# Grouped mixture of experts on one core: the branch to further passes moved behind the last scatter, weight splits ordered ahead of the last copies on ScalarE too, and three of four embedding quarters kept in routing

## The chip, the cores and the metric

The kernel runs on one core of one Trainium2 chip. Its time is the device time of one execution in microseconds (us), and less is better. Before the change it takes 1997.78 us, the median of 3 runs (1997.4 to 1998.72).

The engines are TensorE (PE, with PEld for its weight loads), VectorE (DVE), ScalarE (ACT), GpSimd (POOL) and SyncE (SP, which issues the DMA loads). A "q" behind an engine's name in a profile (PEldq, SPq) means its sequencer: branches, register loads, semaphores and DMA issues, which are not counted as busy.

## What is computed

A float32 network over S = 256 tokens of width D = 1024. A first block of two layers is followed by a second block of four. The change touches only the feed-forward half of the first block's two layers:

```python
for i in range(2):
    mix = ...                       # S5 and pooling in layer 0, attention in layer 1
    x = layer_norm(ALPHA * x + mix, ...)
    ple = (p[i] @ ple_w_proj[i]) * sigmoid(x @ ple_w_gate[i])     # the "embedding"
    ffn = grouped_moe(x, router_w, router_bias, w1[i], w3[i], w2[i])
    x = layer_norm(ALPHA * x + ffn + ple, ...)
```

`grouped_moe` scores 16 experts for each token, chooses a group of four, and in it the two best experts, and adds their `(silu(x w1) * (x w3)) w2`, weighted by the scores. w1 and w3 are 1024 x 512 and w2 is 512 x 1024 for each expert, so a layer reads 96 MB of expert weights.

## The kernel before, in words

**Routing.** `moe` first calls `route` (the scores) and `choose` (L1276), which finds the chosen experts (`Mb`, L1314), counts by five small matmuls (L1318 to L1322) how many tokens each expert has so far, and makes from that each token's `slot` in its expert (L1336, L1337) and its `gates` (L1339 to L1342). An expert takes CAP = 64 tokens in one pass. `choose` also works out the number of passes that the fullest expert needs (`cn`, `npass`, `ni`, L1324 to L1334). `values_load` (L1545) puts `ni` into a register of every engine (one TENSOR_LOAD on each), and `further_passes` (L1596) holds an `If` on it (L1600): a COMPARE_BRANCH on each engine, behind which the loops of the second and later passes stand. With these inputs no further pass is needed, so every engine jumps over them. All this lies ahead of the first expert.

**Embedding.** While routing goes on, PE computes a quarter of the columns of `x @ ple_w_gate` in four pieces of 4 matmuls (`embed`, L1513; one piece is 8 records of the profile), two of them ahead of `choose` and two behind. The tanh and the products behind it are `th` (L1518) on ACT and `pp` (L1521, L1523) on DVE. In this text a piece of 4 is called an embedding quarter.

**Experts.** The 16 experts go in four batches of four. `onehot` (L1349) makes from `slot` the matrix `oh` that selects a batch's tokens; `gather` multiplies it with the tokens (L1363, 16 pairs of records) and copies the result (`xl`, L1365). For each expert `expert_in` does the w1 and w3 products (L1394; its result `h` is copied by ACT, L1397), `expert_act` transposes, takes the silu and the gate (L1405 to L1411). For each pair of experts `pair_out` does the w2 products (L1431) into two halves, copies each half as a high part on ACT (`y`, L1437) and a low part on DVE (L1438), and `scatter` (L1445) adds it to the accumulators `acc` by matmuls. The accumulators are zeroed ahead of the branch by four matmuls (L1543).

**Layer norm.** Behind the last scatter `layer_norm` takes the statistics of `acc` on DVE (L783 to L789, which end in `dg` and `h`); `transpose_part` transposes by PE (L1099), with the bias as a matmul of its own (`bz`, L1092) and matmuls on a tile of ones (L1090) ahead.

**Weights.** Loads of one MB (L109) go into a ring of 16 slots. Three slots are other tiles lent out once: `gb`, `y` and `h`. The next stage's weights are loaded and split ahead of the last scatter by `run_ahead` (L97): each MB is cut in two pieces, and of each piece ACT writes the high part (L122) and DVE the low part (L123). These are 6 splits in layer 0 and 4 in layer 1.

**Order.** A scheduler sets the order of each engine's instructions from priorities; `issue_after(m)` keeps an instruction behind `m`. `run_ahead` returns its last split, `s.split_last`, which is the DVE's, and `pair_out` keeps its last copies behind it: that holds DVE's two `y` copies back, while ACT's two go first. On SP, 14 weight loads are issued ahead of the branch from a list (`s.feed`), the loads into `y`, `gb` and `h` behind it.

Of the kernel before, what the change touches and what calls it, by code (L numbers as in the profile page):

```python
# [8 lines left out]
F32 = mybir.dt.float32  # L9
# [21 lines left out]
class Net:  # L31
    def __init__(s, ctx, tc, ins):
        s.ctx, s.tc, s.nc, s.ins = ctx, tc, tc.nc, ins
        s.right = ctx.enter_context(ExitStack())
        s.slots = [c.enter_context(tc.tile_pool(name="slots" + n, bufs=1, side="right")) for c, n in ((ctx, "a"), (s.right, "b"))]
        s.zpool = None

        s.ahead = deque()

        s.feed = deque()  # L40
# [71 lines left out]
    def split(s, v, to=None):  # L112
# [5 lines left out]
        for i0 in range(0, a, m):  # L118
# [3 lines left out]
            nc.scalar.activation(h, v[:, i0:i0 + n], AF.Copy)  # L122
            s.split_last = nc.vector.tensor_tensor(l, v[:, i0:i0 + n], h.bitcast(F32), op=OP.subtract).ins  # L123
# [1152 lines left out]
    def choose(s, sc, pool, token_rest):  # L1276
# [46 lines left out]
        cn = T([128, 2], "cn")  # L1323
        nc.vector.tensor_reduce(cn[:, 0:1], pr[:, 32:48], axis=AX.X, op=OP.max)  # L1324
        ts(cn[:, 1:2], cn[:, 0:1], 1.0 / CAP, (CAP - 1) / CAP, op0=OP.mult, op1=OP.add)

        npass = T([128, 4], "npass")
        for k in range(3):
            ts(npass[:, k:k + 1], cn[:, 0:1], float(CAP * (k + 1)), None, op0=OP.is_gt)
        tt(npass[:, 0:1], npass[:, 0:1], npass[:, 1:2], op=OP.add)  # L1330
        ts(npass[:, 0:1], npass[:, 0:1], 1.0, None, op0=OP.add)
        tt(npass[:, 0:1], npass[:, 0:1], npass[:, 2:3], op=OP.add)
        ni = T([128, 1], "ni", I32)
        nc.vector.tensor_copy(ni, npass[:, 0:1])  # L1334
# [7 lines left out]
        tt(gates, gates, red[:, :, 0:1].to_broadcast([128, 2, 16]), op=OP.mult)  # L1342
        token_rest(1)
        return gates, slot, ni
# [69 lines left out]
    def pair_out(s, w2, a, wk, last=None, n=2, ahead=None):  # L1414
# [20 lines left out]
        with s.tc.issue_after(ahead()) if ahead else ExitStack():  # L1435
# [51 lines left out]
    def moe(s, i, x, ahead):  # L1487
# [4 lines left out]
        part = lambda w, n, q: w[q * n * 128:(q + 1) * n * 128].rearrange("(a p) n -> p a n", p=128)  # L1492
        both = lambda a, b, n: (lambda q: [s.feed.popleft() if s.feed else s.load(part(w, n, q)) for w in (a, b)])
        with ExitStack() as stack:
# [51 lines left out]
            next(em)  # L1546
            s.further_passes(reg, slot, gates, acc, (w1, w3, w2), pool, wk)
            s.ring["w"].extendleft([gate, lambda: s.hp.tile([128, 2048], F32, name="h"), lambda: pool.tile([128, 2048], F32, name="gb"),
                                    lambda: wk.tile([128, 2048], F32, name="y", bufs=1)])
            nxt = batch(0, oh)  # L1550
            for _ in em:
                pass
            done, acts, y = [], [], None
            for e in range(NE):
# [3 lines left out]
                h = s.expert_in(both(w1[e], w3[e], 4), xg[:, :, q], wk)  # L1558
                if q == 0:
# [24 lines left out]
                if e == 12:  # L1584
                    lnr = s.norm_rows(lnz, pool, False)
# [5 lines left out]
            s.scatter(acc, y, done.pop(0), False, True)  # L1591
            x = s.layer_norm(acc, lnr, True, s.cols["mix_norm"] if i else None)
# [3 lines left out]
    def further_passes(s, reg, slot, gates, acc, w, pool, wk):  # L1596
# [3 lines left out]
        with s.tc.If(reg > 1):  # L1600
            left = wk.tile([128, 2, 16], F32, name="left", bufs=1)
            nc.vector.tensor_copy(left, slot)
            with s.tc.For_i(1, reg):
                nc.vector.tensor_scalar(left, left, float(CAP), None, op0=OP.subtract)
                with s.tc.For_i(0, NE, 2) as e:
                    sl = wk.tile([128, 2, 2, 2], F32, name="sl")
                    nc.vector.tensor_copy(sl[:, 0], left[:, :, bass.ds(e, 2)])
                    nc.vector.tensor_copy(sl[:, 1], gates[:, :, bass.ds(e, 2)])
                    oh = s.onehot(sl[:, 0], s.hp.tile([128, 2048], F32, name="h")[:, :4 * CAP].bitcast(F32R), 2)
                    xg, rest = s.gather(oh, lambda: pool.tile([128, 2048], F32, name="gb")[:, :4 * CAP].rearrange("p (t c) -> p t c", t=2), sl[:, 1], wk)  # L1610
                    oT, gr = rest()

                    def pair(a, b, n):

                        def get(q):
                            m = pool.tile([128, 2048], F32, name="gb").rearrange("p (z a n) -> z p a n", z=2, a=n)
# [370 lines left out]
```

## Time and profile before

| | us |
|---|---|
| median of 3 runs | 1997.78 |
| the profiled execution | 1997.02 |
| its span on the core | 1995.3 |
| TensorE busy in the span | 1943.9 (97%) |
| VectorE busy | 1045.9 (52%) |
| ScalarE busy | 794.0 (40%) |
| GpSimd busy | 90.1 (5%) |

The span is what the trace covers, from the first to the last instruction; the profiled execution's own time is 1.72 us longer, and it lies 0.76 us below the median. The mean granted TensorE clock was 0.99 of full speed. A group of the trace gives its start, its duration, the engine, the line, the operation and tiles, and in square brackets how long the engine stood idle before it and what ended that. Matmuls in float32 are recorded as two records each.

### The profile page before, as it was taken

To read this page: it belongs to the slowest core of one execution; us is meant where nothing else is said; L and a number is where in the kernel's file an instruction comes from. 1 tells how busy PE (TensorE), PEld (TensorE's weight loads), DVE (VectorE), ACT (ScalarE), POOL (GpSimd) and SP (SyncE) were. 2 spreads that over 40 slices of the span, in tenths; PEclk is the share of its full clock that TensorE was granted. 3 is DMA by queue.
4 is the path that set the end of the run, shared out by engine and by line. 5 is a ranking of instruction groups with operands and counts; after the bars stand their busy time and mean duration, and the time that the engine had idled before them with its cause. 6 is when DMAs were issued, how large, how long until landed. Compare 5 with 4: busy or idle time off the path is not lost.

```text
span 1995.3 us, 29243 instructions
## 1 busy us (share of the span) xinstructions
PE 1943.9 (97%) x12088; PEld 1508.1 (76%) x12088; DVE 1045.9 (52%) x1707; ACT 794.0 (40%) x1194; POOL 90.1 (5%) x109
## 2 busy tenths in 40 slices
PE   8999999989999999899999999999999999999999
PEld 6664444378754543499999998999878999999998
DVE  8951111065441111486655698555686555757554
ACT  4321111144321111355444597444655444535442
POOL 5300000000000000000000000000140000000000
PEclk9999999989999999999999999999999999999999
DMA  8559999843679999484655545554453555555540
GB/s 250 186 217 389 390 389 396 307 161 101 207 274 393 389 393 393 141 291 139 222 188 190 174 161 178 190 190 125 151 169 127 190 188 180 180 171 190 184 133 22
DMA packets 271598, 444.34 MB, mean 223 GB/s; under 512 B 14354, under 2 KB 165185, under 8 KB 271457
## 3 DMA queue, kind: packets, MB, share of 16 engines
q1 hardware_dynamic: 270192, 442.30, 63.7%
q8 instruction: 98, 1.61, 0.3%
q14 instruction: 44, 0.35, 0.1%
q10 hardware_dynamic: 1264, 0.09, 0.0%
HBM read 441.30 MB, written 1.05 MB: 222 GB/s over the span
## 4 chain that ended last, share of the span: by engine, by line
PE 64%; DVE 3%; ACT 2%; POOL 1%; issue 1%; DMA 0%; POOLq 0%; ACTq 0%; DVEq 0%; SPq 0%
PE mm L177 11%; PE mm L175 11%; PE mm L176 11%; PE mm L1394 6%; PE acc L175 5%; PE acc L176 5%; PE acc L177 5%; PE mm L1431 3%; PE mm L1513 1%; DVE z L123 1%; PE acc L1445 1%; PE mm L1363 1%; POOL hrs L536 1%; DVE e L417 1%; PE mm L240 0%
## 5 line engine op out<-in xcount | busy, mean ns | idle before, releaser
L123 DVE TENSOR_TENSOR z<-w,z 128x1024 fp32r<-128x1024 f32 (+1 forms) x382 | 453.0, 1204 | 277.7 <-ACT z L122 277.5
L175 PE MATMUL mm<-xh,z 128*128 128x256 f32 x1920 | 540.4, 282 | 0.0
L177 PE MATMUL mm<-xh,z 128*128 128x256 f32 x1920 | 539.0, 281 | 0.4 <-DVE z L123 0.4
L176 PE MATMUL mm<-xl,z 128*128 128x256 f32 x1920 | 538.7, 281 | 0.2
L122 ACT ACTIVATE z<-w 128x1024 fp32r<-128x1024 f32 (+1 forms) x382 | 389.3, 1045 | 288.4 <-PE mm L177 141.3
L175 PEld LDWEIGHTS mm<-xh,z 128*128 128x128 f32 x1920 | 362.1, 189 | 3.4 <-ACT z L122 1.1
L176 PEld LDWEIGHTS mm<-xl,z 128*128 128x128 f32 x1920 | 361.4, 188 | 3.7 <-DVE xl L1121 1.6
L177 PEld LDWEIGHTS mm<-xh,z 128*128 128x128 f32 x1920 | 362.1, 189 | 2.5 <-DVE z L123 2.5
L1394 PE MATMUL mm<-w,xl 128*64 128x512 f32 x1008 | 237.4, 596 | 0.0
L175 PE MATMUL acc<-z,yh 128*128 128x512 f32 x488 | 195.1, 400 | 0.5 <-ACT yh L216 0.5
L176 PE MATMUL acc<-z,yh 128*128 128x512 f32 x488 | 193.7, 397 | 0.0
L177 PE MATMUL acc<-z,yl 128*128 128x512 f32 x488 | 193.0, 397 | 0.0
L1394 PEld LDWEIGHTS mm<-w,xl 128*64 128x64 f32 x1008 | 72.3, 137 | 136.2 <-issue 131.7
L1431 PE MATMUL mm<-w,ea 128*64 128x512 f32 x480 | 121.8, 596 | 0.0
L1397 ACT ACTIVATE h<-mm 128x512 f32<-128x512 f32 x32 | 19.1, 597 | 234.6 <-PE mm L1394 234.6
L177 PEld LDWEIGHTS acc<-z,yl 128*128 128x128 f32 x488 | 91.9, 188 | 22.3 <-DVE yl L684 0.2
L175 PEld LDWEIGHTS acc<-z,yh 128*128 128x128 f32 x488 | 91.9, 188 | 20.3 <-ACT yh L216 0.9
L1438 DVE TENSOR_TENSOR y<-mm,y 128x512 fp32r<-128x512 f32 x32 | 21.7, 687 | 162.3 <-ACT y L1437 162.3
L176 PEld LDWEIGHTS acc<-z,yh 128*128 128x128 f32 x488 | 92.0, 188 | 19.5
L1410 DVE TENSOR_TENSOR eb<-mm,gr 128x256 f32<-128x256 f32 x32 | 13.4, 419 | 160.8 <-ACT ea L1408 160.8
L1431 PEld LDWEIGHTS mm<-w,ea 128*64 128x64 f32 x480 | 39.3, 136 | 70.2 <-issue 66.1
L216 ACT ACTIVATE yh<-e 128x512 fp32r<-128x512 f32 x57 | 36.0, 632 | 120.5 <-DVE e L352 100.6
(512 smaller groups left out, 2401.0 us busy)
## 6 DMA issues: line engine op xcount, KB each, us to landing
w<-in_moe_w_dram SPq DMA_DIRECT2D x182, 1024.0 KB
w<-in_ffn_w_gu_dram SPq DMA_DIRECT2D x88, 1024.0 KB
w<-in_ffn_w_down_dram SPq DMA_DIRECT2D x44, 1024.0 KB
w<-in_conv_w_in_dram SPq DMA_DIRECT2D x24, 1024.0 KB
w<-in_sb_w_qkv_dram SPq DMA_DIRECT2D x12, 1024.0 KB
w<-in_lru_w_in_dram SPq DMA_DIRECT2D x10, 1024.0 KB
w<-in_ple_w_gate_dram SPq DMA_DIRECT2D x8, 1024.0 KB
w<-in_conv_w_out_dram SPq DMA_DIRECT2D x8, 1024.0 KB
```

Of the source, the lines that this page charges most:

```text
L122: nc.scalar.activation(h, v[:, i0:i0 + n], AF.Copy)
L123: s.split_last = nc.vector.tensor_tensor(l, v[:, i0:i0 + n], h.bitcast(F32), op=OP.subtract).ins
L175: mm(o, ah, bh, start=first, stop=False, skip_group_check=True)
L176: mm(o, ah, bl, start=False, stop=False, skip_group_check=True)
L177: mm(o, al, bh, start=False, stop=last, skip_group_check=True)
L216: nc.scalar.activation(hi, src, AF.Copy)
L417: nc.vector.scalar_tensor_tensor(rc[:, n, k:], rs[:, n, :S - k], w(3 - k), rc[:, n, k:], op0=OP.mult, op1=OP.add)
L536: nc.gpsimd.tensor_tensor(rs, ss, s.half[:, :ss.shape[1]], op=OP.pow)
L1363: nc.tensor.matmul(pb[:, k * w:(k + 1) * w], s.tok[i // 2][:, i % 2, c:c + 128], oh[:, i % 2], start=k == 0 and i == 0, stop=i == 3, skip_ ...
L1394: nc.tensor.matmul(pb[z * CAP:(z + 1) * CAP], x[:, q * n + k], w[z][:, k], start=q == 0 and k == 0, stop=q * n + k == KT - 1, skip_group_c ...
L1431: nc.tensor.matmul(pb[hf][p * CAP:(p + 1) * CAP], a[p][:, q * n + f], w[p][:, f, hf * 512:hf * 512 + 512], start=q == 0 and f == 0, stop=q ...
L1438: nc.vector.tensor_tensor(y[1][:, hf], pb[hf], y[0][:, hf].bitcast(F32), op=OP.subtract)
```

## The change

Three parts, the same in both layers.

1. The `If` of `further_passes` stands behind the last scatter, ahead of `layer_norm`. Its loops have buffers of their own kind (`th`, `oh` and `h` where they had `gb` and `h`), and the copy `left` is dropped. The arithmetic for `ni` is done behind the first batch's gather, and `values_load` is written in expert 12. The zeroing matmuls (L1543) go; the first scatter starts the accumulators. `s.feed` goes: the loads into `y`, `gb` and `h` stand in the ring from the start, so they no longer come behind the branch on SP.
2. `split_last` is now a pair of ACT's and DVE's split, and the last `y` copies are kept behind both.
3. One of the two embedding quarters behind `choose`, with the tanh and the products, moves to behind the second expert's w1 and w3 products.

```diff
 def split(s, v, to=None):
-            nc.scalar.activation(h, v[:, i0:i0 + n], AF.Copy)
-            s.split_last = nc.vector.tensor_tensor(l, v[:, i0:i0 + n], h.bitcast(F32), op=OP.subtract).ins
+            s.split_last = (nc.scalar.activation(h, v[:, i0:i0 + n], AF.Copy).ins,
+                            nc.vector.tensor_tensor(l, v[:, i0:i0 + n], h.bitcast(F32), op=OP.subtract).ins)
...
 def choose(s, sc, pool, token_rest):
-        cn = T([128, 2], "cn")
...
-        nc.vector.tensor_copy(ni, npass[:, 0:1])
         slot = T([128, 2, 16], "slot")
...
+        def passes():
+            cn = T([128, 2], "cn")
...
+            return ni
         token_rest(1)
-        return gates, slot, ni
+        return gates, slot, passes
...
 def pair_out(...):
-        with s.tc.issue_after(ahead()) if ahead else ExitStack():
+        with ExitStack() as order:
+            for m in ahead() if ahead else ():
+                order.enter_context(s.tc.issue_after(m))
...
 def moe(s, i, x, ahead):
+            extra = [lambda: pool.tile([128, 2048], F32, name="gb"), lambda: wk.tile([128, 2048], F32, name="y", bufs=1),
+                     lambda: s.hp.tile([128, 2048], F32, name="h")]
             gate = s.ring["w"].pop()
-            order = [(w, 4, q) for e in range(3) for q in range(2) for w in (w1[e], w3[e])] + [(w2[d], 2, 0) for d in range(2)]
-            s.feed.extend([s.load(part(*o)) for o in order])
-            gates, slot, ni = s.choose(sc, pool, token_rest)
+            for k, f in zip((13, 14, 16), extra):
+                s.ring["w"].insert(k, f)
+            gates, slot, passes = s.choose(sc, pool, token_rest)
             oh = hots(0)
-            zero = s.rw.bitcast(BF)[:, :1, 32:].to_broadcast([128, 16, 32])
-            for o in acc:
-                nc.tensor.matmul(o, s.onesb, zero, start=True, stop=False, skip_group_check=True)
             next(em)
-            reg = nc.values_load(ni[0:1, 0:1], min_val=1, max_val=4)
-            next(em)
-            s.further_passes(reg, slot, gates, acc, (w1, w3, w2), pool, wk)
...
             nxt = batch(0, oh)
-            for _ in em:
-                pass
+            ni = passes()
...
-                    s.scatter(acc, y, done.pop(0), False, False)
+                    s.scatter(acc, y, done.pop(0), e == 3, False)
+                if e == 1:
+                    for _ in em:
+                        pass
...
                 if e == 12:
+                    reg = nc.values_load(ni[0:1, 0:1], min_val=1, max_val=4)
...
             s.scatter(acc, y, done.pop(0), False, True)
+            s.further_passes(reg, slot, gates, acc, (w1, w3, w2), pool, wk)
             x = s.layer_norm(acc, lnr, True, s.cols["mix_norm"] if i else None)
```

What that does to the order of instructions shows at three places. In the changed kernel's file the same statements stand a few lines off: L1515 is L1513 of before, L1364 L1363, L1395 L1394, L1432 L1431, L1440 and L1441 L1437 and L1438, L1448 L1445, L120 and L121 L122 and L123, L1088, L1090 and L1097 are L1090, L1092 and L1099, L1584 is L1545 and L1601 is L1600.

TensorE in layer 0's routing, behind the counts, before (the rows of the loops that are jumped over are left out here and below; L1545 and L1600 are the register load and the branch):

```order
L1322 MATMUL mm<-Mb,onesb 128x16
L1513 MATMUL mm<-w_1156,xh 128x256 x8
L1545 TENSOR_LOAD ni
L1600 COMPARE_AND_BRANCH
...
L1600 UNCONDITIONAL_BRANCH
L1363 MATMUL mm<-oh,tokh 128x256 x2
...
L1394 MATMUL mm<-w_1264,xl 64x512
```

And now, with the place of the fourth quarter behind expert 1:

```order
L1320 MATMUL mm<-Mb,onesb 128x16
L1515 MATMUL mm<-w_1156,xh 128x256 x4
L1364 MATMUL mm<-oh,tokh 128x256 x2
...
L1395 MATMUL mm<-w_1375,xl 64x512
...
L1395 MATMUL mm<-w_1441,xl 64x512
L1515 MATMUL mm<-w_1156,xh 128x256 x4
L1406 MATMUL mm<-ident,h_1451 128x128 x4
```

Register load, branch and one quarter no longer stand between the counts and the gather; the quarter stands between expert 1's products and its transposes L1406.

ScalarE at the last copies of layer 0 (`gb` is the layer norm's gain; the two numbers of `w` are the piece written and the MB read), before:

```order
L752 ACTIVATE gb<-mm 128x512
L1437 ACTIVATE y<-mm 128x512 x2
L122 ACTIVATE w_2807<-w_2801 128x1024
L122 ACTIVATE w_2808<-w_2801 128x1024
L122 ACTIVATE w_2813<-w_2803 128x1024
L122 ACTIVATE w_2814<-w_2803 128x1024
L122 ACTIVATE w_2819<-w_2805 128x1024
L122 ACTIVATE w_2820<-w_2805 128x1024
L1106 ACTIVATE xh<-mm 128x4x128 x4
```

And now:

```order
L750 ACTIVATE gb<-mm 128x512
L120 ACTIVATE w_2590<-w_2584 128x1024
L120 ACTIVATE w_2591<-w_2584 128x1024
L120 ACTIVATE w_2596<-w_2586 128x1024
L120 ACTIVATE w_2597<-w_2586 128x1024
L120 ACTIVATE w_2602<-w_2588 128x1024
L120 ACTIVATE w_2603<-w_2588 128x1024
L1440 ACTIVATE y<-mm 128x512 x2
L1584 TENSOR_LOAD ni
L1601 COMPARE_AND_BRANCH
```

The splits stand ahead of both copies, and register load and branch behind them. On DVE the low parts of the splits stood ahead of the two `y` copies before and do now; the register load and the branch are new behind them there too.

TensorE from the last scatter on in layer 0, before:

```order
L1431 MATMUL mm<-w_2786,ea 64x512
L1445 MATMUL acc<-y,oT 128x512 x2
L1431 MATMUL mm<-w_2787,ea 64x512
L1431 MATMUL mm<-w_2786,ea 64x512
L1431 MATMUL mm<-w_2787,ea 64x512
L1445 MATMUL acc<-y,oT 128x512 x6
L1090 MATMUL mm<-ones 128x128 x4
L1099 MATMUL mm<-dg,h 128x128 x8
L1090 MATMUL mm<-ones 128x128 x4
L1092 MATMUL mm<-ind,lnz 128x512 x2
L175 MATMUL acc<-w_2807,xh 128x512
L1099 MATMUL mm<-dg,h 128x128 x8
```

And now:

```order
L1448 MATMUL acc<-y,oT 128x512 x8
L1584 TENSOR_LOAD ni
L1601 COMPARE_AND_BRANCH
...
L1601 UNCONDITIONAL_BRANCH
L1090 MATMUL mm<-ind,lnz 128x512 x2
L1088 MATMUL mm<-ones 128x128 x8
L1090 MATMUL mm<-ind,lnz 128x512 x2
L1097 MATMUL mm<-dg,h 128x128 x8
...
L1097 MATMUL mm<-dg,h 128x128 x8
```

All 16 w2 products stand together ahead of the 8 scatter matmuls, then register load and branch, and all four `bz` and all eight matmuls on ones stand between the branch and the first transposes.

## Rows read from the trace of the kernel before

**Rows 1.** The page: busy time of the engines; the w1/w3 products on TensorE

```profile
PE 1943.9 (97%) x12088; PEld 1508.1 (76%) x12088; DVE 1045.9 (52%) x1707; ACT 794.0 (40%) x1194; POOL 90.1 (5%) x109
...
L1394 PE MATMUL mm<-w,xl 128*64 128x512 f32 x1008 | 237.4, 596 | 0.0
```

**Rows 2.** Timeline of TensorE, layer 0's routing

```profile
134.53 3.70 PE L1513 MATMUL mm<-w,xh 128*128 128x256 f32 x16
141.71 0.77 PE L1363 MATMUL mm<-oh,tokh 128*128 128x256 f32 x2 [3.47 <-DVE th L1377]
...
148.22 1.08 PE L1394 MATMUL mm<-w,xl 128*64 128x512 f32 x4
```

**Rows 3.** Line L1600, the branch: durations in ns (lowest/median/highest), first and last start

```profile
L1600 PEldq COMPARE_BRANCH  x2: 327/1940/3552, 137.8 to 568.7; - x2
L1600 DVEq COMPARE_BRANCH  x2: 56/64/72, 137.9 to 568.6; - x2
```

**Rows 4.** Layer 0's gather: busy PE, PEld, DVE, ACT, POOL; clock; DMA share, GB/s

```profile
142.00:144.00 2.00, 2.00 (x11) 2.00 (x11) 0.00 (x0) 0.15 (x1) 0.00 (x0) 0.50 0.39 146
```

**Rows 5.** Timeline of VectorE in layer 0's routing, the first batch's second one-hot

```profile
136.53 0.42 DVE L1349 TENSOR_TENSOR oh<-iota,slot 128x256 fp32r<-128x256 f32 x1
```

**Rows 6.** Timeline of TensorE, layer 1's routing

```profile
565.55 3.70 PE L1513 MATMUL mm<-w,xh 128*128 128x256 f32 x16
569.98 0.50 PE L1363 MATMUL mm<-oh,tokh 128*128 128x256 f32 x2 [0.73 <-ACTq L1600]
...
573.94 1.51 PE L1394 MATMUL mm<-w,xl 128*64 128x512 f32 x6
```

**Rows 7.** Timeline of TensorE, expert 1 of layer 0

```profile
165.00 0.66 PE L1405 MATMUL mm<-ident,h 128*128 128x128 f32 x4 [0.79 <-ACT h L1397]
```

**Rows 8.** Timeline of TensorE, end of layer 0's experts

```profile
388.02 1.93 PE L1431 MATMUL mm<-w,ea 128*64 128x512 f32 x4
...
396.58 0.73 PE L1445 MATMUL acc<-y,oT 128*128 128x512 f32 x2 [0.69 <-ACT y L1437]
397.24 1.93 PE L1431 MATMUL mm<-w,ea 128*64 128x512 f32 x6
...
408.34 2.25 PE L1445 MATMUL acc<-y,oT 128*128 128x512 f32 x4 [7.75 <-DVE y L1438]
...
414.66 1.06 PE L1090 MATMUL mm<-ones 128*128 128x128 f32 x8
415.65 0.73 PE L1092 MATMUL mm<-ind,lnz 36*128 36x512 f32 x2
...
416.65 1.95 PE L1099 MATMUL mm<-dg,h 128*128 128x128 f32 x16
```

**Rows 9.** Timeline of ScalarE, end of layer 0's experts

```profile
388.13 0.60 ACT L752 ACTIVATE gb<-mm 128x512 f32<-128x512 f32 x1
...
399.70 5.78 ACT L122 ACTIVATE w<-w 128x1024 fp32r<-128x1024 f32 x6
```

**Rows 10.** Timeline of VectorE, end of layer 0's experts

```profile
400.78 6.90 DVE L123 TENSOR_TENSOR w<-w,w 128x1024 fp32r<-128x1024 f32 x6 [11.78 <-ACT w L122]
407.60 1.28 DVE L1438 TENSOR_TENSOR y<-mm,y 128x512 fp32r<-128x512 f32 x2
...
415.14 0.75 DVE L789 SCALAR_TENSOR_TENSOR h<-acc,mv,gb 128x512 f32<-128x512 f32 x1
```

**Rows 11.** Timeline of VectorE, end of layer 1's experts

```profile
826.56 4.63 DVE L123 TENSOR_TENSOR w<-w,w 128x1024 fp32r<-128x1024 f32 x4 [11.79 <-ACT w L122]
831.11 1.28 DVE L1438 TENSOR_TENSOR y<-mm,y 128x512 fp32r<-128x512 f32 x2
```

**Rows 12.** Timeline of TensorE, layer 1's last pair of experts

```profile
813.80 1.93 PE L1431 MATMUL mm<-w,ea 128*64 128x512 f32 x4
```

**Rows 13.** The same, a window behind layer 0's last weight loads

```profile
378.00:380.00 2.00, 2.00 (x7) 0.53 (x7) 0.00 (x0) 0.00 (x0) 0.00 (x0) 1.00 0.00 0
```

**Rows 14.** Tile `ni`: its register load on TensorE's sequencer, ns

```profile
L1545 PEldq TENSOR_LOAD <-ni x2: 313/402/492, 137.2 to 568.3; - x2
```

More of the change, by code (lines that the diff above doesn't have):

```diff
@@ L1322, in choose @@
         mm(pr[:, 32:48], s.onesb, Mb[:, 1], start=False, stop=True)
-        cn = T([128, 2], "cn")
[L1324 to L1333, printed above, removed]
-        nc.vector.tensor_copy(ni, npass[:, 0:1])
         slot = T([128, 2, 16], "slot")
@@ L1342, in choose @@
         tt(gates, gates, red[:, :, 0:1].to_broadcast([128, 2, 16]), op=OP.mult)
+        def passes():
+            cn = T([128, 2], "cn")
+            nc.vector.tensor_reduce(cn[:, 0:1], pr[:, 32:48], axis=AX.X, op=OP.max)
+            ts(cn[:, 1:2], cn[:, 0:1], 1.0 / CAP, (CAP - 1) / CAP, op0=OP.mult, op1=OP.add)
+            npass = T([128, 4], "npass")
+            for k in range(3):
+                ts(npass[:, k:k + 1], cn[:, 0:1], float(CAP * (k + 1)), None, op0=OP.is_gt)
+            tt(npass[:, 0:1], npass[:, 0:1], npass[:, 1:2], op=OP.add)
+            ts(npass[:, 0:1], npass[:, 0:1], 1.0, None, op0=OP.add)
+            tt(npass[:, 0:1], npass[:, 0:1], npass[:, 2:3], op=OP.add)
+            ni = T([128, 1], "ni", I32)
+            nc.vector.tensor_copy(ni, npass[:, 0:1])
+            return ni
         token_rest(1)
-        return gates, slot, ni
+        return gates, slot, passes
     def onehot(s, slot, oh, ne):
@@ L1490, in moe @@
         w1, w3, w2 = (ins["moe_w%d" % k][i] for k in (1, 3, 2))
-        part = lambda w, n, q: w[q * n * 128:(q + 1) * n * 128].rearrange("(a p) n -> p a n", p=128)
-        both = lambda a, b, n: (lambda q: [s.feed.popleft() if s.feed else s.load(part(w, n, q)) for w in (a, b)])
+        both = lambda a, b, n: (lambda q: [s.load(w[q * n * 128:(q + 1) * n * 128].rearrange("(a p) n -> p a n", p=128)) for w in (a, b)])
         with ExitStack() as stack:
@@ L1558, in moe @@
                 h = s.expert_in(both(w1[e], w3[e], 4), xg[:, :, q], wk)
+                if e == 2:
+                    s.ring["w"].append(gate)
                 if q == 0:
@@ L1600, in further_passes @@
         with s.tc.If(reg > 1):
-            left = wk.tile([128, 2, 16], F32, name="left", bufs=1)
-            nc.vector.tensor_copy(left, slot)
             with s.tc.For_i(1, reg):
-                nc.vector.tensor_scalar(left, left, float(CAP), None, op0=OP.subtract)
+                nc.vector.tensor_scalar(slot, slot, float(CAP), None, op0=OP.subtract)
                 with s.tc.For_i(0, NE, 2) as e:
                     sl = wk.tile([128, 2, 2, 2], F32, name="sl")
-                    nc.vector.tensor_copy(sl[:, 0], left[:, :, bass.ds(e, 2)])
+                    nc.vector.tensor_copy(sl[:, 0], slot[:, :, bass.ds(e, 2)])
                     nc.vector.tensor_copy(sl[:, 1], gates[:, :, bass.ds(e, 2)])
-                    oh = s.onehot(sl[:, 0], s.hp.tile([128, 2048], F32, name="h")[:, :4 * CAP].bitcast(F32R), 2)
-                    xg, rest = s.gather(oh, lambda: pool.tile([128, 2048], F32, name="gb")[:, :4 * CAP].rearrange("p (t c) -> p t c", t=2), sl[:, 1], wk)
+                    oh = s.onehot(sl[:, 0], wk.tile([128, 2 * NB * CAP], F32R, name="oh", bufs=1)[:, :4 * CAP], 2)
+                    xg, rest = s.gather(oh, lambda: pool.tile([128, 2, NB * CAP], F32, name="th")[:, :, :2 * CAP], sl[:, 1], wk)
                     oT, gr = rest()
@@ L1615, in get @@
                         def get(q):
[L1616 removed]
+                            m = s.hp.tile([128, 2048], F32, name="h").rearrange("p (z a n) -> z p a n", z=2, a=n)
                             for z, w in enumerate((a, b)):
```

3 lines of the change are left out of this document (removed).

## The prediction

> **What bounds the kernel now.** I read the page first: TensorE is busy 97% of the span [rows 1], so nearly all that can be won is the 51 us in which it stands, and the time in which it works at a low clock. Then I read the timelines of TensorE, VectorE and ScalarE at the two places where the change moves instructions, in both layers, since what an edit is worth there depends on which wait ends last.
>
> Place one is routing. In layer 0 TensorE ends its second group of embedding matmuls at 138.23 and starts the gather only at 141.71 [rows 2]. The row names a wait for `th` on DVE, but the line of the branch shows what held it: TensorE's COMPARE_BRANCH took 3552 ns in one layer and 327 in the other [rows 3], and 137.8 + 3.55 is 141.4, just ahead of the gather. [...] In layer 1 the branch took 0.33, the gap is 0.73 and the gather takes 573.94 - 569.98 = 3.96 [rows 6], which I use as its duration at full clock.
>
> Place two is the end of the experts. TensorE is done with the last w2 products of layer 0 at 397.24 + 1.93 = 399.2, then stands 7.75 us for DVE's `y` [rows 8]. That `y` is late because DVE's six splits stand ahead of it [rows 10]; these wait 11.78 us for ACT's splits, and ACT starts those at 399.70, behind its own `y` copies [rows 9], although the DMA queues are empty at 378 to 380 [rows 13], so that the weights to be split are there. A chain of four links: last product, ACT copy, ACT split, DVE split. Layer 1 has the same with four splits [rows 11].
>
> **Part 3 and the branch out of routing.** Layer 0: one embedding quarter is half of the 3.70 us row, so the third ends at 134.53 + 1.85 = 136.4 [rows 2]. The gather then needs the second one-hot, which ends at 136.95 [rows 5]; seven small DVE operations for `ni` leave the stretch ahead of it, each overlapped by others, so I take 136.75. The gap on TensorE is then 0.4 instead of 3.47 us, and I expect the clock to stay up, as it did over layer 1's gap of 0.73. Gather 3.96: the first expert starts at 140.7 instead of 148.22, **-7.5**. The fourth quarter comes back behind expert 1, 1.85 us, but TensorE waits 0.79 there for `h` [rows 7], which it fills: **+1.06** (bounds 0 and 1.85). Layer 1: quarter to 567.4, one-hot at the same distance as in layer 0 to 567.8, gather to 571.75 instead of 573.94 [rows 6], **-2.2**, and +1.06 for the quarter. The removed zeroing matmuls and the DVE work for `ni` ran beside other work; I cost both at nothing. Routing together: **-7.6**, bounds -9.7 (quarters wholly hidden) and -6.0 (not hidden).
>
> **Part 2, the splits first on ACT.** Let T be the end of DVE's last `y` copy. Before, T = 407.60 + 1.28 = 408.88 [rows 10]. Now ACT is free for splits at 388.13 + 0.60 = 388.7 [rows 9]. One split is 5.78 / 6 = 0.96, so DVE starts at 389.7, needs 6.90, and its two copies 1.28: 397.9. The other condition is TensorE's w2 products: from 388.02 to 399.17 they took 11.15 [rows 8], and in that lie one scatter pair (0.66 to the next start), its wait (0.69), and one pair of bias matmuls of the same shape (0.65), all of which now stand behind. That leaves 9.15; with the second half's ACT copy (0.60) and DVE copy (0.64) T is 398.4 if no w2 products overlap better. I take 398.1: **-10.8** (bounds -10.5 and -11.0). ACT's own `y` copies are not held back, since its six splits end at 388.7 + 5.8 = 394.5. Layer 1 has two splits fewer, so TensorE's products set it: the same 10.1 us behind their start at 813.80 [rows 12] is 823.9, instead of 831.11 + 1.28 = 832.39 [rows 11]: **-8.5** (bounds -8.1 and -9.4, the latter if the products' first rows, which ran singly ahead of the bias pair, overlap).
>
> **Part 1, the branch ahead of the layer norm.** Before, TensorE's second transposes of layer 0 end at 416.65 + 1.95 = 418.6 = T + 9.7 [rows 8]. Now behind the last scatter pair (0.7) come TensorE's register load (0.3 to 0.5) [rows 14] and the branch (0.33 where it is short) [rows 3]: TensorE is free at T + 1.45. Then four bias matmuls and eight on ones stand ahead of the first transposes, twice 0.65 and twice 1.0 [rows 8], 3.3 us: the first transposes start at T + 4.8 and end at T + 6.8. The second ones need `h`, which DVE ended at 415.89 = T + 7.0 [rows 10]; its own register load and branch add some 0.3 (0.06 of it the branch [rows 3]). They end at T + 7.3 + 1.95 = T + 9.25: **-0.4** in layer 0, where a low clock had slowed them, and I take **-0.3** in layer 1. So TensorE's branch is hidden behind DVE's statistics by about half a microsecond. ACT pays its own there too, with nothing due. SP's later weight loads now come behind its branch; SP reads the register long before, and the loads that go out first are those whose splits come first. That the loads into `y`, `gb` and `h` go out ahead of routing costs nothing that I can see: TensorE never waited on weights in any expert (idle 0.0 ahead of L1394) [rows 1].
>
> **Sum.** -7.6 - 10.8 - 8.5 - 0.4 - 0.3 = **-27.6** against the profiled execution's 1997.02: 1969.4. That execution lies 0.76 below the median of the runs, so the median should be **1970.2**.
>
> **The rivals.** (A) *The long branch moves along.* The 3552 ns of layer 0 do not go but turn up at one or both of the new places. The row shows one long and one short branch for the same jump over the same loops, so what makes it long is where it falls in the instruction stream, and that changes. TensorE is then free at T + 4.65, the first transposes start at T + 8.0, and the second end at T + 12.0 instead of 9.25: +2.7. If the stand of over 3 us also lowers the clock, as it did in routing [rows 4], the twelve small matmuls and the transposes take up to twice as long, some +5. One long branch gives 1973 to 1975, both 1976 to 1980. For: nothing in the rows says where the jump lands. Against: only one of two was long.
> [...]
>
> (B) *Routing's gain is given back.* The experts start 6.5 us earlier in layer 0, but weights come at the pace of the queues. If they were just in time, TensorE would wait for them and all of -7.6 would go: 1977.8. Against: the 0.0 of rows 1, and the queues' empty stretch at 378 [rows 13], over 8 us ahead of the last w2 products at 388.
>
> (C) *Slower: ACT's queue is blocked.* A split waits for its load; with the splits ahead of the copies, a late load now holds ACT's `y`, the scatter and TensorE one for one. T is the landing plus 0.96 + 1.15 + 1.28 = 3.4. It turns into a loss at a landing of 405.5, over 25 us later than rows 13 show. Forty later in both layers would be T + 12.5 twice: 1997.8 - 7.6 + 25 - 0.7 = 2014.5. Against: the empty queues of rows 13.
>
> (D) *No change.* The ends' gain comes back as a wait on something else that was due at the old T, which the rows don't show, and routing's with it: within 0.2% of 1997.8. The order of instructions does show the splits, the quarter and the branch where the change puts them.
>
> **How the numbers follow.** Forecast 0.70, A 0.14, B 0.09, C 0.03, D 0.04. The best bounds of all terms give -9.7 - 11.0 - 9.4 - 1.0 = -31.1, that is 1966.7; the worst likely, A at both ends or B, 1977 to 1980. The range is 1966 to 1979; it leaves out C, D and the far end of A. 0.2%, about 4 us, is what a measurement of this kernel can tell from no change. Faster by more: forecast, A and B, 0.93; within: D, 0.04; slower: C, 0.03.
>
> **What the next profile would show.** First w1 matmul of layer 0 near 140.7 and no window at 0.50 in the gather; expert 1's gap gone; at the end of each layer's experts ACT splits starting 0.1 us behind the `gb` copy and TensorE's wait ahead of the last scatter pairs at about 1 us instead of layer 0's 7.75; TensorE's COMPARE_BRANCH at 0.3 us twice; first transposes 4.8 us behind DVE's last `y`. The prediction is wrong if a branch of over 3 us shows there, if the experts wait for weights, or if ACT's splits start late.

## The result and the profile after

The changed kernel takes 1972.3 us, the median of 4 runs (1971.94 to 1973.08); the kernel before, 1997.59 (1997.31 to 1998.72, 4 runs). The ratio is 0.9873, 95% interval 0.9856 to 0.989: faster, by 25.3 us. The forecast was 1970.2 in a range of 1966 to 1979.

Where it went is best read by stages. I took the same marks from the timelines of both traces: the first count matmul (L1318 before, L1316 after), the first w1 matmul, the first w2 matmul of the last pair, T (the end of DVE's last `y` copy), the start of the first transposes and the end of the second ones. The lengths, in us, worked out from those rows (a table of mine, not a view):

```
                          before     after   difference
start to first count      134.40    135.62      +1.22
layer 0: to first w1       13.82      6.14      -7.68
         to last pair     239.80    239.69      -0.11
         to T              20.86      9.78     -11.08
         to transposes      3.20      4.68      +1.48
         to their end       6.51      4.87      -1.64
attention to first count  146.82    146.47      -0.35
layer 1: to first w1        8.53      6.03      -2.50
         to last pair     239.86    239.58      -0.28
         to T              18.59      9.48      -9.11
         to transposes      3.20      9.09      +5.89
         to their end       6.15      5.36      -0.79
```

The rest, the second block, differs by 0.4 us, and the sum is that of the spans, 1995.3 to 1970.7. The 1.22 us ahead of the first count is no part of the change: the same mark lies between 134.3 and 137.1 in the other traces of this study, whatever the kernel.

The page of the changed kernel, against [rows 1]: TensorE's busy time fell by 9 us, 2.4 of them in layer 0's gather (6.5 to 4.1 us) and about as many from the order of the scatter matmuls at expert 9 (below); its idle time fell by the rest.

```profile
span 1970.7 us, 29221 instructions
...
PE 1934.6 (98%) x12080; PEld 1507.7 (77%) x12080; DVE 1045.7 (53%) x1707; ACT 794.4 (40%) x1194; POOL 91.0 (5%) x109
```

TensorE's timeline in layer 0's routing and at expert 1, against [rows 2, 7]:

```profile
135.75 1.97 PE L1515 MATMUL mm<-w,xh 128*128 128x256 f32 x8
137.66 0.63 PE L1364 MATMUL mm<-oh,tokh 128*128 128x256 f32 x2
...
141.75 7.09 PE L1395 MATMUL mm<-w,xl 128*64 128x512 f32 x32
...
157.68 2.00 PE L1515 MATMUL mm<-w,xh 128*128 128x256 f32 x8
159.51 0.60 PE L1406 MATMUL mm<-ident,h 128*128 128x128 f32 x4
```

The gather follows the third quarter at once, takes 4.1 us at the full clock (granted 1.00 from 136 to 142), and expert 1's gap of 0.79 us is filled.

The end of layer 0's experts on TensorE, against [rows 8]:

```profile
381.44 8.12 PE L1432 MATMUL mm<-w,ea 128*64 128x512 f32 x32
...
390.24 2.00 PE L1448 MATMUL acc<-y,oT 128*128 128x512 f32 x7 [0.26 <-ACT y L1440]
392.63 0.70 PE L1090 MATMUL mm<-ind,lnz 36*128 36x512 f32 x2 [0.39 <-PEq L1601]
...
395.90 2.05 PE L1097 MATMUL mm<-dg,h 128*128 128x128 f32 x16
...
398.72 2.05 PE L1097 MATMUL mm<-dg,h 128*128 128x128 f32 x16 [0.24 <-DVE dg L786]
```

and its splits and copies on ScalarE and VectorE, against [rows 9, 10]:

```profile
382.04 5.78 ACT L120 ACTIVATE w<-w 128x1024 fp32r<-128x1024 f32 x6
```

```profile
383.12 6.90 DVE L121 TENSOR_TENSOR w<-w,w 128x1024 fp32r<-128x1024 f32 x6 [0.70 <-ACT w L120]
389.94 1.28 DVE L1441 TENSOR_TENSOR y<-mm,y 128x512 fp32r<-128x512 f32 x2
...
392.46 1.29 DVE L781 BATCH_NORM_STATS2 bn<-acc 128x6 f32<-128x512 f32 x2 [1.24 <-PEq L1601]
```

The wait of 7.75 us is gone. The branch costs TensorE 0.39 us where it stands, and the second transposes wait 0.24 us for DVE. DVE itself is later by the branch: its statistics wait 1.24 us for a signal that TensorE gives at its branch, where they waited 0.29 for the last scatter before. So the branch is not hidden behind DVE's statistics; it stands ahead of them.

Layer 1 is another matter. TensorE behind its branch, and DVE at the same place:

```profile
803.86 0.69 PE L1090 MATMUL mm<-ind,lnz 36*128 36x512 f32 x2 [0.30 <-PEq L1601]
804.48 2.05 PE L1088 MATMUL mm<-ones 128*128 128x128 f32 x16
809.66 0.62 PE L1090 MATMUL mm<-ind,lnz 36*128 36x512 f32 x2 [3.13 <-issue]
811.42 5.36 PE L1097 MATMUL mm<-dg,h 128*128 128x128 f32 x32 [1.14 <-DVE dg L786]
```

```profile
805.27 0.15 DVE L783 TENSOR_SCALAR mv<-mv 128x1 f32<-128x1 f32 x1
810.42 0.75 DVE L785 SCALAR_TENSOR_TENSOR h<-acc,mv,gb 128x512 f32<-128x512 f32 x1 [5.00 <-SPq L1601]
```

Two new waits: DVE stands 5.00 us for SP's part of the branch before it may write `h`, and TensorE 3.13 us for nothing that a semaphore shows ("issue"). DVE's ends last: the transposes wait another 1.14 us for its `dg`. The granted clock is 0.50 from 812 to 814, and the 32 transpose records take 5.36 us instead of twice 2.05. The branch itself, by engine (ns, lowest/median/highest, first and last start), and SP's loads just ahead of it:

```profile
L1601 SPq EVENT_SEMAPHORE  x16: 17/17/17, 381.6 to 810.2; - x16
...
L1601 SPq COMPARE_BRANCH  x2: 50/52/53, 380.1 to 801.2; - x2
...
L1601 PEldq COMPARE_BRANCH  x2: 330/388/445, 391.9 to 802.8; - x2
```

```profile
797.57 13.19 SPq L107 DMA_DIRECT2D w<-in_conv_w_in_dram  x4
```

TensorE's branches are short. SP branched at 801.2, but its last semaphore signal is at 810.2, and three 1 MB loads were on their way from 797.6 on.

### The profile page after: what moved, and what is told of

The parts are those of the page before. It is cut to its first block, busy times and chain, and to the rows that moved or that the text cites. A ratio compares the mean times of both kernels' runs of the same rounds, so it can differ in the third digit from the quotient of the medians.

```text
span 1970.7 us, 29221 instructions
## 1 busy us (share of the span) xinstructions
PE 1934.6 (98%) x12080; PEld 1507.7 (77%) x12080; DVE 1045.7 (53%) x1707; ACT 794.4 (40%) x1194; POOL 91.0 (5%) x109
## 4 chain that ended last, share of the span: by engine, by line
PE 51%; DVE 3%; ACT 1%; POOL 1%; issue 1%; DMA 0%; POOLq 0%; DVEq 0%; ACTq 0%; SPq 0%
PE mm L173 11%; PE mm L174 11%; PE mm L175 11%; PE acc L173 6%; PE acc L174 6%; PE acc L175 6%; DVE z L121 1%; POOL hrs L534 1%; DVE e L415 1%; PE mm L238 0%; ACT z L120 0%; POOL q L612 0%; POOL kv L612 0%; DMA w<-in_lru_w_out_dram 0%; ACT xh L1118 0%
## 5 line engine op out<-in xcount | busy, mean ns | idle before, releaser
L121 DVE TENSOR_TENSOR z<-w,z 128x1024 fp32r<-128x1024 f32 (+1 forms) x382 | 453.3, 1205 | 277.8 <-ACT z L120 277.6
L120 ACT ACTIVATE z<-w 128x1024 fp32r<-128x1024 f32 (+1 forms) x382 | 389.2, 1045 | 287.9 <-PE mm L175 134.2
L1395 PE MATMUL mm<-w,xl 128*64 128x512 f32 x1008 | 235.3, 596 | 0.0
L1395 PEld LDWEIGHTS mm<-w,xl 128*64 128x64 f32 x1008 | 71.9, 137 | 135.5 <-issue 132.3
L1432 PE MATMUL mm<-w,ea 128*64 128x512 f32 x480 | 126.5, 595 | 0.0
L1441 DVE TENSOR_TENSOR y<-mm,y 128x512 fp32r<-128x512 f32 x32 | 21.8, 688 | 159.8 <-ACT y L1440 158.8
L1432 PEld LDWEIGHTS mm<-w,ea 128*64 128x64 f32 x480 | 44.3, 137 | 67.1 <-issue 60.2
```

The lines of the kernel that those rows point to most:

```text
L120: s.split_last = (nc.scalar.activation(h, v[:, i0:i0 + n], AF.Copy).ins, nc.vector.tensor_tensor(l, v[:, i0:i0 + n], h.bitcast(F32), op=OP ...
L1395: nc.tensor.matmul(pb[z * CAP:(z + 1) * CAP], x[:, q * n + k], w[z][:, k], start=q == 0 and k == 0, stop=q * n + k == KT - 1, skip_group_c ...
L1432: nc.tensor.matmul(pb[hf][p * CAP:(p + 1) * CAP], a[p][:, q * n + f], w[p][:, f, hf * 512:hf * 512 + 512], start=q == 0 and f == 0, stop=q ...
L1441: nc.vector.tensor_tensor(y[1][:, hf], pb[hf], y[0][:, hf].bitcast(F32), op=OP.subtract)
```

## The experiments

In the longer series the kernel before itself spread from 1990.5 to 1999.8 us, more than some of the differences, so the experiments are judged first by the lengths of the stages in their traces. Equal work mostly agrees there to 0.2 us, but not where the clock falls: the end of layer 1 takes 14.45 us behind T in one trace of the changed kernel and 15.70 in the other (e8_after); the clock is at 0.50 until 814 in the first and past 816 in the second. Those lengths behind T, and the total of the runs (the first two lines are the kernels themselves, e8_after is the changed kernel once more; the labels stand at the experiments):

```
                 T to transposes / to their end    median us (runs)
                    layer 0        layer 1
before            3.20 / 9.71    3.20 /  9.36      1997.59 (4)
after             4.68 / 9.55    9.09 / 14.45      1972.3  (4)
e8_after          4.68 / 9.56    9.08 / 15.70      1972.36 (5)
e1_y_buffer       4.68 / 9.41    7.86 / 13.32      1969.53 (4)
e3_no_if          3.11 / 8.48    3.12 /  8.47      1971.25 (4)
p2_only           3.13 / 8.51    3.14 /  8.50      1977.35 (4)
no_p2             6.70 / 12.18   6.39 / 10.99      1988.33 (10)
e4_hold           4.68 / 9.41    4.80 /  9.50      1967.71 (4)
e5_short          4.67 / 9.40    4.78 /  9.51      1967.5  (1)
e6_long           4.67 / 9.40   12.79 / 16.63      1973.89 (1)
e7_hold_h         4.68 / 9.56    4.79 /  9.63      1970.16 (4)
e9_hold           4.68 / 9.41    4.79 /  9.50      1970.02 (4)
e10_hold_early    4.69 / 9.41    4.81 /  9.50      1970.39 (4)
no_p3             4.68 / 9.55    8.95 / 15.43      1974.67 (4)
```

**Part 2 alone** (p2_only). The kernel before with `split_last` as the pair and `pair_out` behind both, as in the diff of the change.

> The kernel before with only the order of the splits changed (ACT's and DVE's ahead of the last copies). Theory: T moves by -10.8 us in layer 0 and by -8.5 to -9 in layer 1, the clock stays up behind it, and nothing of the branch stands there, so both layers keep it: 1997.6 - 20 = 1977.5 us. Rival (part of layer 1's gain is lost to something else that was due late, not to the branch): layer 1 keeps only some 4 us, 1982.

Measured: 1977.35. From the first w2 matmul of the last pair to the end of the second transposes it takes 19.48 and 19.46 us, before 30.57 and 27.95: -11.1 and -8.5. The theory holds, and layer 1 keeps its gain where no branch stands behind it; the rival falls.

**Parts 1 and 3 alone** (no_p2).

```diff
-            for m in ahead() if ahead else ():
+            for m in ahead()[1:] if ahead else ():
```

> The changed kernel with the last copies kept behind DVE's splits only, as before: what parts 1 and 3 do alone. Theory: routing gains 7.7 + 2.5 and the experts 0.2 each, the ends pay the branch, 0.5 to 1.5 each; T comes so late that the loads in flight on SP have landed by then and DVE does not wait for SP: 1997.6 - 10.5 + 2 = 1989 us. Rival (the wait for SP comes with the branch wherever T lies): layer 1 loses some 5 more, 1993 to 1994.

Measured: 1988.33. Routing gains 7.7 and 2.5, the ends lose 1.0 and 0.15 against before. DVE does not wait for SP here. By the lengths of the stages, part 2 alone makes 11.1 + 8.5 = 19.6 us, parts 1 and 3 alone 9.5 (routing 7.7 + 2.5, experts 0.1 + 0.3, ends -1.0 - 0.15), together 29; in one kernel they make 25.8. The difference is the end of layer 1, where the lengths of the parts make 19.6 us (19.46 + 0.15) and the changed kernel takes 23.93; the end of layer 0 gives 1.1 back (19.33 instead of 19.48 + 1.0). In the changed kernel TensorE branches at 802.8 and SP's last signal is at 810.2; here TensorE branches at 822.6 and SP's last signal is at 824.2, so the loads are nearly done. The clock is at 0.50 here too (818 to 828), and the 16 records on ones take 3.43 us where they take 2.05 in the changed kernel, so that TensorE also comes to its next instructions later; the two are not told apart.

**No branch at all** (e3_no_if).

```diff
-                    reg = nc.values_load(ni[0:1, 0:1], min_val=1, max_val=4)
-            s.further_passes(reg, slot, gates, acc, (w1, w3, w2), pool, wk)
```

> The changed kernel without the branch and the loops behind it (the second and later passes are left out; with these inputs none is needed), so the two ends show what the branch costs. Theory: layer 0's end gains about 0.5 us (TensorE's branch is nearly hidden behind DVE's statistics), layer 1's about 5, by both stalls: 1966.5 us. Rival (the branch is cheap and layer 1 lost its time to the loads themselves): within 1 us of 1972.3.

Measured: medians don't tell. The four runs lie at 1967.0, 1967.2, 1975.3 and 1978.5, and in the trace, which is of the third, the granted clock is 0.50 from 1438 to 1454, in the second block, where of the other traces only e7_hold_h's has it. The ends do tell: from the last pair's first w2 matmul to the end of the second transposes, 19.44 us in layer 0 against 19.33 with the branch, and 19.43 against 23.93 in layer 1. The branch costs layer 1 4.5 us, by this trace of the changed kernel, and layer 0 nothing, where 0.5 was expected: 1.1 us more behind T, where DVE's statistics wait 1.24 us instead of 0.31, and 1.2 less ahead of it. Without the branch the scheduler again puts a pair of the layer norm's bias matmuls behind the first four records of the last w2 products, as in the kernel before (10.96 us to T instead of 9.78).

**Another buffer for the loops that don't run** (e1_y_buffer).

```diff
-                            m = s.hp.tile([128, 2048], F32, name="h").rearrange("p (z a n) -> z p a n", z=2, a=n)
+                            m = wk.tile([128, 2048], F32, name="y", bufs=1).rearrange("p (z a n) -> z p a n", z=2, a=n)
```

> The changed kernel, but the never-run loops read their weights into the tile y instead of h, so the layer norm's first write to h no longer has to wait for SP's part of the branch. Theory (SP's branch comes behind three weight loads in flight in layer 1 and DVE waits for it): the wait of 5.0 us on DVE ahead of L785 in layer 1 goes; the stall of 3.1 us on TensorE between the matmuls on ones and the second bias pair stays, since nothing on SP holds it, and the second transposes end some 2.5 us earlier: 1969.8 us. Rival 1 (TensorE's stall alone sets the end): DVE's wait goes and the time stays at 1972.3. Rival 2 (both stalls have one cause, the loads in flight): both go, 1967.6 or less.

Measured: 1969.53. DVE and TensorE in layer 1:

```profile
803.83 0.74 DVE L785 SCALAR_TENSOR_TENSOR h<-acc,mv,gb 128x512 f32<-128x512 f32 x1
```

```profile
802.99 2.05 PE L1088 MATMUL mm<-ones 128*128 128x128 f32 x16
808.14 0.63 PE L1090 MATMUL mm<-ind,lnz 36*128 36x512 f32 x2 [3.11 <-issue]
808.71 5.47 PE L1097 MATMUL mm<-dg,h 128*128 128x128 f32 x32
```

DVE's wait is gone, TensorE's stays, and the end comes 1.1 us earlier behind T than in the first trace of the changed kernel and 2.4 earlier than in the second (15.70); 2.5 was expected. The two stalls overlapped, and a low clock behind TensorE's own stall stays (0.50 from 810 to 812). Two waits, then, and the second is TensorE's.

**Nothing in flight at the branch** (e4_hold). On the y buffer, three loads held back by a one-element clear on DVE behind the layer norm's first `dg` (six loads carry the clear).

```diff
+        if s.hold:
+            s.hold -= 1
+            with s.tc.issue_after(s.ln_dve0):
+                s.nc.vector.memset(v[:1, 0, :1], 0.0)
         s.nc.sync.dma_start(v, src)
...
+                if t == 0:
+                    s.ln_dve0 = last
...
+        s.hold = 6
```

> The run with the y buffer, and the next stage's weight loads of layer 1 that went out ahead of SP's branch held back until behind it: DVE clears one element of each behind the layer norm's first dg, so no load is in flight while TensorE branches. Theory (TensorE's stall of 3.1 us is the fetch of its next instructions, which waits behind the loads in flight): the stall goes, the second transposes end 9.3 to 9.5 us behind T instead of 13.3, and if the loads that now start some 5 us later are still in time, 1965.6 us. Rival (the stall hangs on the place of the branch's target alone): it stays at 3.1 us, the end at 13.3 behind T, 1969.5 or more.

**The branch's target moved**, nearer and further, by leaving out or doubling products in loops that don't run.

```diff
-  ... for p in range(2)]
+  ... for p in ((0,) if s.late else (0, 1))]             # e5_short
+  ... for p in ((0, 1, 0, 1) if s.late else (0, 1))]     # e6_long
+  acts = (acts * 2)[-2:]                                 # both
```

Each of these two was run once.

> The run with the y buffer, with the never-run loops of layer 1 shortened by one expert's products, so that TensorE's branch there jumps to a place 75 instruction words nearer (what is left out is not needed with these inputs). Place theory: TensorE's stall of 3.1 us in layer 1 goes, some 4 us. Loads theory: it stays at 3.1 us and the time at 1969.5.

> The run with the y buffer, with the never-run loops of layer 1 lengthened by two experts' products, so that the branch jumps 148 instruction words further. [...] Loads theory: branch 0.33 and a stall of 3.1 us as in the run with the y buffer.

Measured, TensorE behind layer 1's branch in the held run:

```profile
802.93 2.05 PE L1095 MATMUL mm<-ones 128*128 128x128 f32 x16
805.06 0.61 PE L1097 MATMUL mm<-ind,lnz 36*128 36x512 f32 x2
805.60 2.05 PE L1104 MATMUL mm<-dg,h 128*128 128x128 f32 x16
```

with the nearer target:

```profile
804.63 2.05 PE L1088 MATMUL mm<-ones 128*128 128x128 f32 x16
806.62 0.73 PE L1090 MATMUL mm<-ind,lnz 36*128 36x512 f32 x2
```

and with the further one, line of the branch, then timeline:

```profile
L1602 PEldq COMPARE_BRANCH  x2: 445/3568/6690, 390.4 to 801.3; - x2
```

```profile
808.30 1.19 PE L1090 MATMUL mm<-ind,lnz 36*128 36x512 f32 x2 [6.27 <-PEq L1602]
```

The stall goes in both of the first two: neither the place theory nor the loads theory is the whole; in these runs the stall takes both conditions. The DMA view shows how they can join. In the changed kernel, the queues from TensorE's branch to the end of its stand (kind of queue, packets, MB, share of time), first 802.8 to 806.5, then 806.5 to 808.5:

```profile
q1 hardware_dynamic: 1258, 1.27, 107.8%
q14 instruction: 2, 0.02, 1.3%
...
q1 hardware_dynamic: 506, 0.50, 80.6%
q8 instruction: 1, 0.02, 3.7%
```

and in the held run, 802.6 to 804.0:

```profile
q8 instruction: 1, 0.02, 3.9%
```

One 16 KB packet of instructions (queue q8) comes about 4 us behind the branch with the loads in flight (at 806.8), and 1.5 us behind it without (802.8, the branch at 801.3). With the nearer target it also came 4 us behind (at 807.0, the branch at 803.0), but TensorE had instructions left until then. So the stall reads as a fetch that is late because of the loads and needed early because of the place. That the packet is TensorE's is an inference from two things. The stand ends 2.9 us behind the packet's start in the changed kernel (806.8 to 809.66) and in the run with the y buffer (805.3 to 808.14). And q8's packets go with TensorE's instructions: the page of the changed kernel has

```profile
q8 instruction: 98, 1.61, 0.3%
```

98 packets for 24,160 matmuls and weight loads, one for some 247; all other engines together have about 3,000 instructions there.

The further target made the branch itself last 6.69 us, where TensorE's two take 0.33 and 0.45 in the run with the y buffer, and the kernel was 1973.89. That bears out the prediction's rival A as a mechanism: the target was moved, and the jump got long. In the changed kernel, with its target where it is, the two take 0.45 and 0.33 us. What it is about a target's place that makes a jump long is not shown. The price was not the 3.55 us of [rows 3], which rival A moves along, but 6.69, with loads in flight.

**The buffer h, nothing in flight** (e7_hold_h). The changed kernel with the clears alone.

> The changed kernel with its own buffer h in the never-run loops, and the three weight loads held back until behind SP's branch as in the held run. Theory (DVE's wait of 5.0 us was for SP, which signals its queues' semaphores only when the loads in flight have landed): with nothing in flight SP signals at once, DVE's wait and TensorE's stall both go, and the end of layer 1 is that of the held run, second transposes 9.4 to 9.5 us behind T: 1967.7 us. Rival (the wait comes with the buffer h, whatever SP has in flight): DVE waits on, and the end is 11 us or more behind T.

Measured: behind T the end is at 9.63 us, as with the y buffer. DVE's write of `h` waits 0.23 us:

```profile
804.89 0.75 DVE L790 SCALAR_TENSOR_TENSOR h<-acc,mv,gb 128x512 f32<-128x512 f32 x1 [0.23 <-issue]
```

```profile
L1608 SPq EVENT_SEMAPHORE  x16: 17/17/17, 381.0 to 783.0; - x16
...
L1608 SPq COMPARE_BRANCH  x2: 50/52/53, 379.4 to 775.3; - x2
```

But SP did not signal at once. With the held loads behind it, SP reaches its branch 26 us earlier (775.3 instead of 801.2), and its last signal again comes 7.7 us behind it, only that nothing waits for it at 783.0. So this run does not tell the loads in flight from SP's being late. The landings in the traces do. In layer 1 of the changed kernel the last packet of the three loads lands at 810.16 and SP's last signal follows at 810.17. In layer 0 SP branches at 380.1 with three loads in flight as well; they land at 381.56, 384.61 and 388.50, SP signals at 381.58, 384.62 and 388.52 and is done at 388.9. At these four SP signals a queue's semaphore within 0.02 us of the landing of that queue's load, and DVE's write of `h` starts behind the last of the eight (810.42). Layer 0 has the same wait on SP and loses nothing, since SP is done there over 5 us ahead of DVE's write of `h` (394.42). One thing stays open: in layer 1 SP's first signal comes 5.8 us behind its branch, with the loads held or not, though that queue's load had landed 5 us before it and more.

The total, 1970.16 (1968.24 to 1976.62), is less clear than the trace, which is of the slowest run and has the clock at 0.50 from 1438 to 1458.

**Part 3 undone** (no_p3).

```diff
+            for _ in em:
+                pass
             nxt = batch(0, oh)
...
-                if e == 1:
-                    for _ in em:
-                        pass
```

> The changed kernel with the fourth embedding quarter back ahead of the first gather. Theory: routing is 1.85 us longer in each layer, expert 1 is 0.9 shorter with its gap of 0.79 back, so 1972.3 + 1.9 = 1974.2 us. Rival (the quarter costs the experts as much as it saves in routing): 1972.3.

Measured: 1974.67 (1972.52 to 1975.63). In the traces routing is 1.27 and 1.37 us longer to the first w1 matmul, the experts 1.04 and 0.91 shorter: part 3 is worth 0.2 to 0.5 us a layer, not 0.9. The median is near the forecast of 1974.2 by chance: of the 3.2 us between the two traces, 1.4 lie ahead of the first count and 1.0 at the end of layer 1, where the two traces of the changed kernel differ by 1.2 themselves. Of the 1.85 us a quarter, 0.5 is not won. In this trace two quarters take 3.34 us up to the gather, so one is 1.67; the rest goes mostly at the gather's start, which with three quarters comes as the one-hot does (its weight load stands 0.32 us before it).

**The versions that beat both** (the changed kernel again as e8_after, the held one again as e9_hold, and e10_hold_early).

> The changed kernel itself again, on the same chip as the held version, so that the two can be compared: 1972 us, with DVE's wait of 5.0 and TensorE's stall of 3.1 in layer 1.

> The held version with the y buffer again, beside the changed kernel on the same chip: 4.3 to 5 us less than that, 1967.5 us.

> The held version with the y buffer, with its one-element clears on four loads only (not six) and the first two behind the layer norm's first aggregate instead of its first dg, so that the loads start sooner after the branch and no clear waits for TensorE later. Theory: branch and instruction fetch still find the queues empty, the second transposes end 9.4 to 9.5 us behind T, and of the 1 to 2 us that the held version gave back in the second block at least half is kept: 1967 us or less. Rival (the fetch now meets the loads again): TensorE's stall comes back in part, the end is 10 to 13 behind T, 1968 to 1970.

Measured on one chip: 1972.36 (1970.73 to 1973.48) for the changed kernel, 1970.02 (1967.72 to 1970.83) for the held one, which had 1967.71 in its own series (e4_hold, 1965.6 expected); the third, on its own, 1970.39 (1968.08 to 1972.15). So holding gains 2.3 us on one chip, not 4.3 to 5, and the third misses its 1967, though its end of layer 1 is as expected. Layer 1's end is 5 to 6 us shorter in all held runs, but their second block is 1 to 4 us longer in three of them (1151.7, 1152.4 and 1154.3 against 1150.0 and 1150.6 in the two traces of the changed kernel) and some 10 us in e7_hold_h, with its stretch at half clock. Why the three are longer is not shown. That the weights come later would be a reason, but in the second block TensorE waits for split weights (tile `z`) only 2.1 us in e10_hold_early, 0.7 in e9_hold and at most 1.1 in e4_hold, against 0.4 in the changed kernel, and e10_hold_early's clock falls as well (0.56 from 828 to 830). The y buffer alone gives nothing back (1150.6). Its 2.8 us by the medians are across chips, and the median of the kernel before differs there by 3.4 us, so what is shown of its gain is the end of layer 1. Holding the loads gains 2.3 us on one chip, 4.6 across chips; which of the two is best stays open.

## Why the prediction was right, point by point

- **Routing** (-7.5 and -2.2 to the first w1 matmul): -7.68 and -2.50. The long branch and the half clock were there to be had, as rows 2 to 4 said; the clock stayed up (granted 1.00 from 136 to 142). The length of layer 0's stretch to the first w1 matmul varies: p2_only, with the same routing as before, takes 12.62 us there and not 13.82, so up to 1.2 of the 7.68 us may be chance.
- **The fourth quarter** (+1.06 a layer): +0.93 at expert 1 in layer 0 (165.58 - 148.22 = 17.36 before, 160.04 - 141.75 = 18.29 after). But the experts as a whole did not get longer. Between experts 8 and 9 the scheduler had put three records of scatter matmuls among the w1/w3 products of the kernel before, which cost 1.2 us in each layer (10.19 against 8.97), and the changed order no longer does. The rows of the kernel before show it at expert 9; the prediction read only the ends and routing.

```profile
276.27 4.50 PE L1394 MATMUL mm<-w,xl 128*64 128x512 f32 x18
280.71 0.98 PE L1445 MATMUL acc<-y,oT 128*128 128x512 f32 x3
281.62 3.65 PE L1394 MATMUL mm<-w,xl 128*64 128x512 f32 x14
285.19 1.43 PE L1445 MATMUL acc<-y,oT 128*128 128x512 f32 x5
```

```profile
270.86 7.09 PE L1395 MATMUL mm<-w,xl 128*64 128x512 f32 x32
277.87 2.12 PE L1448 MATMUL acc<-y,oT 128*128 128x512 f32 x8
```

- **T** (-10.8 and -8.5): -11.08 and -9.11, measured from the last pair's start. In layer 0 DVE's splits set it, 0.3 us tighter than I took; in layer 1 the w2 products, 8.1 us in one piece where the working had 9.15.
- **Behind T, layer 0** (transposes at T + 4.8, end at T + 9.25): 4.68 and 9.55. The reason given is wrong in part: TensorE's branch is not hidden behind DVE's statistics, which wait 1.24 us for TensorE's signal there. The end comes 0.3 us later than forecast.
- **Behind T, layer 1** (-0.3): this step failed; it is +5.1 (14.45 against 9.36). The sentence that failed is that SP's loads "come behind its branch; SP reads the register long before": three of them go ahead of it, SP's last signal comes as the last of them lands (810.17 and 810.16), and layer norm's `h` is a buffer of the never-run loops, so that DVE waits 5.00 us for SP. The second clause is true (SP loads its register at 550.9) and beside the point: it is when SP reaches the branch, and what it then has in flight, that counts. In layer 0 SP is there 11 us ahead of T, in layer 1 only 1.1. TensorE's stand of 3.13 us, read above as a fetch that is late behind the same loads, is the second half.
- **The sum**: -27.6 forecast, -25.3 measured. The failed step alone makes 1970.2 + 5.4 = 1975.6, which is still inside the range, since the range allowed for a long branch at one end. That the median came within 2.1 us of the forecast is luck: the experts gave 2.5 us that nobody had counted (+2.1 forecast, -0.4 measured, mostly by the scatter's order), and T 0.9 in both layers.
- **Rival A** was right as a mechanism (e6_long, 6.69 us with the target moved) and did not come to pass (0.45 and 0.33 us in the changed kernel); TensorE's stand of 3.13 us is by the reading above a milder form of it. Its price, +2.7 to 5 a layer, is about what layer 1 lost, but the wait that ends last there, DVE's for SP, is not in it. **D**'s mechanism came true in part: 5.1 of the 9.1 us won at T in layer 1 came back as a wait on something else, which rows of before did not show; the other gains stayed. **B** and **C** fell: experts as long as before, and splits starting with the end of the `gb` copy.

## What to carry to other kernels

In this kernel the branch over code that never runs was a meeting point for the engines that signal in it (in layer 1 DVE's statistics waited 1.36 us for TensorE's signal, its write of `h` 5.00 us for SP's), and for a buffer that the code names: with `y` in the place of `h` the 5.00 us went. So ask of each engine what it has in flight when it reaches such a branch, SP's loads above all (three of 1 MB here), and who next writes a buffer that the skipped code would have used; give that code a buffer with no user close behind. When a wait is cut ahead of such a place, look at what now arrives there early: the two edits were worth 29 us apart and 25.8 together, by the lengths of the stages.

## What was not expected of the hardware

- SP's 16 semaphore signals at the branches take 17 ns each, but the last one of layer 1 came 9 us behind SP's branch (801.2 to 810.2), as the last of 3 MB of loads in flight landed. In layer 0 it came 8.8 us behind (380.1 to 388.9), and nothing waited for it.
- TensorE's jump over loops that don't run took 0.32 to 0.45 us, 3.55, or 6.69. Moving the target, in e6_long, made the last of these; whether the loads in flight make the difference between 3.55 and 6.69 is not shown.
- A 16 KB packet of instructions came 1.0 to 1.5 us behind TensorE's branch with no loads in flight (e9_hold, e4_hold) and 4 us behind layer 1's with three (e1_y_buffer, e5_short and the changed kernel).
- Three records of scatter matmuls within an expert's products (128*64 in their rows) cost 1.2 us more than the same records behind them, in both layers (10.19 against 8.97 us in layer 0, 10.18 against 8.98 in layer 1).
